# The opening of a decoder step: an early table load, matmuls on zeros, split weight pieces and two key tiles built side by side

## Chip, cores and metric

The kernel is one program on one core of a Trainium2 chip. Its five engines run their own instruction streams and meet at semaphores: TensorE (PE, the matmuls, with its weight loads as PEld), VectorE (DVE), ScalarE (ACT), GpSimd (POOL) and SyncE (SP, which here issues every DMA). The metric is the device time of one execution in microseconds (us); less is better.

## The reference, cut to what matters

One inference step of a trunk of two layers: 512 prompt tokens and 8 sequences of 8 new tokens, 576 tokens in all, with a model width of 1024. Layer 0 mixes tokens by sparse attention with three branches, layer 1 by a gated recurrence; each layer ends with an MLP and a gated projection. All matrices are in float32. The change touches only the first steps: the first norm and the first projections, the keys.

```python
def rmsnorm(x, g):
    xf = x.astype(jnp.float32)
    y = xf * lax.rsqrt(jnp.mean(xf * xf, axis=-1, keepdims=True) + RMS_EPS)
    return (y * g.astype(jnp.float32)).astype(x.dtype)
...
def nsa_project(h, pos, w_in):
    q, kv, gl = jnp.split(h @ w_in, [Q_DIM, Q_DIM + 6 * KV_DIM], axis=-1)
    q = rope(q.reshape(B, T, N_HEADS, HEAD_DIM), pos)
    kv = kv.reshape(B, T, 3, 2, KV_HEADS, HEAD_DIM)
    k = rope(kv[:, :, :, 0].reshape(B, T, 3 * KV_HEADS, HEAD_DIM), pos)
```

## The kernel before

**Layout.** The residual x lies transposed in SBUF as `X`, 8 tiles of 128 features by 576 tokens. A float32 product is made of three passes on numbers of lower precision: every operand is split into a high part (rounded on ACT) and a low part (the rest, by a subtraction on DVE), and a matmul adds hi·hi, hi·lo and lo·hi. `dense_steps` (L236 to L260) does this for one output tile of 128 columns: for each of 8 feature tiles k it issues six passes of 288 tokens, L251 for `wh`·`xh`, L254 for `wh`·`xl` and L257 for `wl`·`xh`. One output tile is 48 passes.

**Weights.** `piece` (L218) loads one 128x1024 block into `wr` (4 buffers), rounds it into `wh` on ACT (L212) and subtracts into `wl` (L229); `wh` and `wl` have 3 buffers each.

**The norm.** `norm_parts` (L327) makes `xh` on ACT (L332) and `xl` on DVE (L333) from `X` times the gain. `norm_square` squares on ACT (L342) and adds the squares into `ssq` (L344) on the engine that it is told. The factor 1/rms itself is not needed for the matmuls: it is applied to their results. It comes in two steps that are held in a list `late` and called between matmuls. `norm_sums` (L349) adds over the features by small matmuls (L355) and forms `RT`, the factor per token, by 12 short DVE instructions (L357, L321 to L326). `norm_spread` (L360) builds diagonal matrices on DVE and POOL (L370, L372), multiplies them by ones on PE (L373, L374), and copies the result to `R` on ACT (L375, L376).

**The key tiles.** The loop at L562 makes eight output tiles, m = 0 to 7, in pairs: compressed keys, compressed values, selected keys, window keys. Their results lie in PSUM in pair buffers `d`, of which there are three here. A finished tile is read out by `k_out`: values are multiplied by `R` (L464); keys go through `rope_out`, which copies quarters on ACT (L452), multiplies by the cosine table on DVE (L453), by the sine table on POOL (L454) and adds (L455). Both tables have first been multiplied by `R` on POOL (L568). So no key tile can leave PSUM before the spread norm is there.

**What sets the order.** The program is recorded in the order of the code, and a scheduler that goes by estimated times then places the instructions of each engine; buffers of a pool are handed out in that same estimate. Each engine runs its list strictly in order. SP issues DMAs in order too, over 8 completion semaphores in turn: a ninth DMA waits until the first has landed.

Of the kernel before, what the change touches and what calls it, by code (L numbers as in the profile page):

```python
# [39 lines left out]
BL = 1, 6  # L40
MID = 4
B0 = 3, 2
MAGIC = 0x5F3759DF


# [129 lines left out]
def program(tc, A, O):  # L175
# [20 lines left out]
    def pair():  # L196
        return psum["d"].tile([128, 2, 512], F32, name="d")

    def bank():
        return psum["s"].tile([128, 512], F32, name="s")  # L200
# [7 lines left out]
    def load(out, src):  # L208
        return nc.sync.dma_start(out, src)
# [7 lines left out]
    def piece(src, shape=(8, 128), lo_on=None, keep=None):  # L217

        n = int(np.prod(shape))
        raw = wp.tile([128, WCOL], F32, name="wr", bufs=4)  # L220
        if keep is not None:
            hi, lo = keep[:, :n], keep[:, n:2 * n]
        else:
            hi = wp.tile([128, WCOL], F32R, name="wh")
            lo = wp.tile([128, WCOL], F32R, name="wl")
        rs = raw[:, :n]
        load(rs, src)
        split_hi(hi[:, :n], rs)
        (lo_on or V).tensor_tensor(lo[:, :n], rs, hi[:, :n].bitcast(F32), op=OP.subtract)  # L229
        pat = "p (a b) -> p a b" if len(shape) == 2 else "p (a b c) -> p a b c"  # L230
        kw = dict(zip("abc", shape))
        return hi[:, :n].rearrange(pat, **kw), lo[:, :n].rearrange(pat, **kw)
# [27 lines left out]
    def dense(hi, lo, xh, xl, mid=None):  # L260

        o = pair()
        for k, _ in enumerate(dense_steps(hi, lo, xh, xl, (o[:, 0, :H2], o[:, 1, :H2]), pin=mid)):
            if k == mid:
                late()
        late()
        return o[:, :, :H2]
# [28 lines left out]
    X = hold["X"]  # L296
    gains = cst.tile([128, 7, KT], F32, name="gains")
    load(gains, A["gains"])
    load(X[:, 0], A["x"][:, 0])
    first = [piece(A["w_k"][0])]  # L300
    for k in range(1, KT):
        load(X[:, k], A["x"][:, k])
        if k == 2:
            first.append(piece(A["w_k"][1]))
    con = cst.tile([128, CONST.shape[1]], F32, name="con")
    C = lambda n: con[:, OFF[n][0]:OFF[n][0] + OFF[n][1]]
    ident = C("ident")
# [27 lines left out]
    def norm_square(m, on):  # L335

        X = hold["X"]
        if m == 0:
            sq = hold["ssq"] = cst.tile([128, NT], F32, name="ssq")
        else:  # L340
            sq = tmp.tile([128, NT], F32, name="t")
        S.activation(sq, X[:, m], AF.Square)  # L342
        if m:
            on.tensor_tensor(hold["ssq"], hold["ssq"], sq, op=OP.add)  # L344
# [42 lines left out]
    load(con, A["const"])  # L387
    V.tensor_copy(identb, ident)
    for m in range(KT):
        norm_square(m, G if m in (1, 4, 7) else V)  # L390
    norm_end()
    hold["late"].insert(0, lambda: None)

    def out_steps(src, oh, ol, ks, got, single=False):

# [29 lines left out]
    def nsa(after):  # L425
# [29 lines left out]
            on.tensor_tensor(out, t1, sw, op=OP.add)  # L455

        def k_proj(m):
            return dense(*(first[m] if m < 2 else piece(A["w_k"][m])), xh, xl, 1 if m == 1 else None)

        def k_out(p, out, rot):  # L460
            if rot:
# [97 lines left out]
        loads = comp_load(cd)  # L559
        outs = [(t[:, m], name) for t, name in ((kC, "o_kc"), (vC, "o_vc"), (kS, "o_ks"), (kW, "o_kw")) for m in range(2)]  # L560
        wait = []
        for m, (out, name) in enumerate(outs):  # L562
            wait.append((k_proj(m), out, name, m % 2))
            for _ in range((0, 0, 3, 3, 3, 3, 3, 1)[m]):
                next(loads, None)
            if m == 1:
                for i in range(2):
                    G.tensor_tensor(rope[:, i], rope[:, i], R, op=OP.mult)  # L568
            while wait and not hold["late"]:
                p, out, name, i = wait.pop(0)  # L570
                k_out(p, out, name != "o_vc")
                store(O[name][:, i], out)
# [975 lines left out]
```

## Time and profile before

| | us |
|---|---|
| median of 3 runs | 1835.22 |
| lowest, highest | 1832.96, 1835.82 |
| the profiled execution | 1833.71 |
| its span, first to last instruction | 1831.9 |
| PE busy in the span | 1768.1 (97%) |
| DVE, ACT, POOL busy | 971.0, 714.2, 479.7 |

The profile is of one execution, so its times are compared with its own 1833.71 us: 1.8 us lie outside the span. A timeline row gives the start, the duration, the engine, the source line, the operation with the tile written and the tiles read, the shape, the number of merged instructions, and in brackets how long the engine was idle before and what ended that. Matmuls overlap: two rows of PE that start 0.13 us apart may each last 0.30 us, so the distance between starts is the price of one.

### The profile page before, as it was taken

The page shows a single profiled execution, that of the slowest core. Times are in us where ns is not written, and L with a number is a line of the kernel's source. Part 1 is how long each engine was busy: PE and PEld are TensorE (multiplying, and loading weights), DVE is VectorE, ACT ScalarE, POOL GpSimd, SP SyncE. Part 2 cuts the span into 40 slices and gives each one's busy share as a digit, 9 for nine tenths or more (in the row PEclk, how much of TensorE's full clock was granted, in tenths as well). Part 3 has the DMA queues.
Part 4 walks back from the last instruction along what each step waited for, and adds up shares of the span by engine and source line. Part 5 has one row for each costly group of instructions (what it writes and reads, how often), then busy time and mean ns, then how long its engine had stood idle before and what let it go on. Part 6 is the DMA issues. An engine that isn't in the chain of part 4 may idle for free.

```text
span 1831.9 us, 31929 instructions
## 1 busy us (share of the span) xinstructions
PE 1768.1 (97%) x13016; PEld 1695.2 (93%) x13016; DVE 971.0 (53%) x1671; ACT 714.2 (39%) x1333; POOL 479.7 (26%) x463
## 2 busy tenths in 40 slices
PE   7999888989999999999999999999999999999997
PEld 7898777779999999999999999999899999999997
DVE  7644777665433334345666757667563333334564
ACT  5556687664332232313432323233243223131442
POOL 3536666652221110202112111211142102020121
PEclk9999999999999999999999999999999999999998
DMA  8333112313222222223231222221132222222311
GB/s 291 128 107 92 35 47 79 113 53 121 81 81 83 91 81 81 82 84 102 88 102 60 82 72 84 81 67 62 39 116 86 86 83 81 81 88 85 115 39 52
DMA packets 64917, 159.42 MB, mean 87 GB/s; under 512 B 8706, under 2 KB 26690, under 8 KB 64770
## 3 DMA queue, kind: packets, MB, share of 16 engines
q1 hardware_dynamic: 64770, 157.38, 26.9%
q8 instruction: 102, 1.67, 0.4%
q14 instruction: 45, 0.37, 0.1%
HBM read 142.33 MB, written 15.02 MB: 86 GB/s over the span
## 4 chain that ended last, share of the span: by engine, by line
PE 88%; DVE 5%; ACT 3%; DMA 1%; issue 1%; POOL 1%; SPq 0%; DVEq 0%; ACTq 0%; POOLq 0%
PE d L251 21%; PE d L254 21%; PE d L257 21%; PE s L1160 2%; PE s L889 1%; PE s L1404 1%; PE s L1408 1%; PE s L1407 1%; PE s L1227 1%; PE s L762 1%; PE s L1222 1%; PE s L845 1%; PE d L1042 1%; PE d L1043 1%; DMA wr<-p_g 1%
## 5 line engine op out<-in xcount | busy, mean ns | idle before, releaser
L212 ACT ACTIVATE wh<-wr 128x1024 fp32r<-128x1024 f32 (+3 forms) x227 | 231.8, 1023 | 764.9 <-PE d L254 635.7
L251 PE MATMUL d<-xh,wh 128*128 128x288 f32 x1776 | 506.1, 299 | 9.9 <-ACT wh L212 7.8
L254 PE MATMUL d<-xl,wh 128*128 128x288 f32 x1776 | 502.6, 298 | 1.9 <-DVE xl L333 1.9
L257 PE MATMUL d<-xh,wl 128*128 128x288 f32 x1776 | 385.2, 297 | 0.3 <-DVE wl L229 0.3
L229 DVE TENSOR_TENSOR wl<-wr,wh 128x1024 fp32r<-128x1024 f32 (+3 forms) x209 | 250.5, 1199 | 243.1 <-ACT wh L212 241.6
L251 PEld LDWEIGHTS d<-xh,wh 128*128 128x128 f32 x1776 | 335.8, 189 | 12.2 <-ACT wh L212 7.8
L254 PEld LDWEIGHTS d<-xl,wh 128*128 128x128 f32 x1776 | 336.1, 189 | 4.8 <-DVE xl L333 3.2
L257 PEld LDWEIGHTS d<-xh,wl 128*128 128x128 f32 x1776 | 286.8, 189 | 1.8 <-DVE wl L229 0.9
L251 PE MATMUL d<-hh,wh 128*128 128x288 f32 x1024 | 287.1, 295 | 0.0
L254 PE MATMUL d<-hl,wh 128*128 128x288 f32 x1024 | 286.8, 295 | 0.0
L1322 POOL TENSOR_TENSOR t<-t 128x576 f32<-128x576 f32 x64 | 104.8, 1637 | 504.0 <-ACT t L1320 504.0
L257 PE MATMUL d<-hh,wl 128*128 128x288 f32 x1024 | 217.9, 294 | 0.0
L254 PEld LDWEIGHTS d<-hl,wh 128*128 128x128 f32 x1024 | 192.4, 188 | 0.0
L251 PEld LDWEIGHTS d<-hh,wh 128*128 128x128 f32 x1024 | 192.3, 188 | 0.0
L257 PEld LDWEIGHTS d<-hh,wl 128*128 128x128 f32 x1024 | 164.2, 188 | 0.0
L1331 DVE TENSOR_TENSOR t<-d,R 128x576 f32<-128x576 f32 x64 | 48.5, 758 | 201.1 <-PE d L257 201.1
L344 POOL TENSOR_TENSOR ssq<-ssq,t 128x576 f32<-128x576 f32 x33 | 54.7, 1658 | 286.8 <-ACT t L342 283.4
L806 POOL TENSOR_SCALAR Eb<-Eb,sm,gate 128x512 f32<-128x512 f32 (+3 forms) x128 | 77.2, 620 | 35.9 <-DVE sm L852 22.8
L215 DVE TENSOR_TENSOR hl<-t,hh 128x576 fp32r<-128x576 f32 x64 | 48.6, 759 | 64.7 <-POOL t L1322 63.7
L1176 POOL TENSOR_TENSOR k<-k,T 128x256 f32<-128x256 f32 (+1 forms) x48 | 34.9, 728 | 183.0 <-PE s L1160 110.1
L850 ACT ACTIVATE Eb<-s,mx 128x512 f32<-128x512 f32 (+2 forms) x96 | 55.2, 582 | 30.5 <-DVE mx L848 29.1
L215 DVE TENSOR_TENSOR pl<-s,ph 128x512 fp32r<-128x512 f32 x80 | 53.1, 684 | 21.5 <-ACT ph L212 21.4
(398 smaller groups left out, 3180.2 us busy)
## 6 DMA issues: line engine op xcount, KB each, us to landing
wr<-w SPq DMA_DIRECT2D x128, 512.0 KB
wr<-p_g SPq DMA_DIRECT2D x16, 512.0 KB
X<-x SPq DMA_DIRECT2D x16, 288.0 KB
wr<-w_k SPq DMA_DIRECT2D x8, 512.0 KB
cd<-cache SPq DMA_DIRECT2D x16, 256.0 KB
wr<-w_c SPq DMA_DIRECT2D x8, 512.0 KB
wr<-w_q SPq DMA_DIRECT2D x8, 512.0 KB
wr<-w_o SPq DMA_DIRECT2D x8, 512.0 KB
```

Source lines behind the costliest of these rows:

```text
L212: S.activation(out, src, AF.Copy, **({} if scale is None else {"scale": scale}))
L215: (on or V).tensor_tensor(out, src, hi.bitcast(F32), op=OP.subtract)
L229: (lo_on or V).tensor_tensor(lo[:, :n], rs, hi[:, :n].bitcast(F32), op=OP.subtract)
L251: z = T.matmul(out[h], hi[:, k], xh[:, k, sl], start=k == 0, stop=False)
L254: T.matmul(out[h], hi[:, k], xl[:, k, sl], start=False, stop=False)
L257: T.matmul(out[h], lo[:, k], xh[:, k, sl], start=False, stop=k == nk - 1)
L344: on.tensor_tensor(hold["ssq"], hold["ssq"], sq, op=OP.add)
L806: G.tensor_scalar(e, e, r, gt3[:, j, h, 1 + br:2 + br], op0=OP.mult, op1=OP.mult)
L850: S.activation(E[:, r, :W], s[:, r - r0, :W], AF.Exp, bias=mx[:, r:r + 1], accum_out=sm[:, r:r + 1])
L1160: T.matmul(p[r, o // 2:e // 2], k[:, o:e], blk(q[:, o:e])[:, :, 1], start=True, stop=True)
L1322: G.tensor_tensor(r2, r, r, op=OP.mult)
L1331: V.tensor_tensor(two(t), p, two(R2), op=OP.mult)
```

## The change

Five edits, all ahead of the fourth key tile.

1. A tile `idle` of 128x512 bfloat16 is set to zero on DVE and multiplied by itself 11 times on PE (L305 of the new file), into a PSUM bank that nothing reads.
2. ACT copies one number (`dry`), so that its table is loaded ahead of the first wait for an input.
3. The first two weight pieces are loaded, rounded and subtracted in two halves of 512 columns (`halves`); the first halves of both come right behind the first tile of `X`, the second halves behind the third.
4. All additions into `ssq` go to DVE; three of seven were on POOL.
5. Key tiles 0 and 1 are computed together, feature tile by feature tile, into two pair buffers. `norm_sums` is called after them and `norm_spread` inside tile 2, behind its fifth feature tile; before, they were called inside and behind tile 1.

```diff
+    idle = tmp.tile([128, 512], BF, name="t")
+    V.memset(idle, 0.0)
+    z = bank()
+    for _ in range(WARM):
+        T.matmul(z, idle[:, :128], idle, start=True, stop=True)
+    dry = small.tile([128, 1], F32, name="dry")
+    G.memset(dry, 0.0)
+    S.activation(dry, dry, AF.Copy)
+    def halves(src):
+        raw = wp.tile([128, WCOL], F32, name="wr", bufs=4)
+        hi, lo = [wp.tile([128, WCOL], F32R, name=n) for n in ("wh", "wl")]
+        for i in range(2):
+            cs = slice(i * 512, i * 512 + 512)
+            load(raw[:, cs], src.rearrange("p k n -> p (k n)")[:, cs])
+            split_hi(hi[:, cs], raw[:, cs])
+            split_lo(lo[:, cs], raw[:, cs], hi[:, cs])
+            yield
...
+    parts = [halves(A["w_k"][m]) for m in range(2)]
     load(X[:, 0], A["x"][:, 0])
-    first = [piece(A["w_k"][0])]
     for k in range(1, KT):
+        if k in (1, 3):
+            next(parts[0])
+            next(parts[1])
         load(X[:, k], A["x"][:, k])
-        if k == 2:
-            first.append(piece(A["w_k"][1]))
...
-        norm_square(m, G if m in (1, 4, 7) else V)
+        norm_square(m, V)
     norm_end()
-    hold["late"].insert(0, lambda: None)
...
-            return dense(*(first[m] if m < 2 else piece(A["w_k"][m])), xh, xl, 1 if m == 1 else None)
+            return dense(*piece(A["w_k"][m]), xh, xl, 4 if m == 2 else None)
...
+        early = [pair() for _ in range(2)]
+        steps = [dense_steps(*first[m], xh, xl, (z[:, 0, :H2], z[:, 1, :H2])) for m, z in enumerate(early)]
+        for _ in range(KT):
+            for z in steps:
+                next(z)
+        late()
         for m, (out, name) in enumerate(outs):
-            wait.append((k_proj(m), out, name, m % 2))
+            wait.append((early[m][:, :, :H2] if m < 2 else k_proj(m), out, name, m % 2))
-            if m == 1:
+            if m == 2:
                 for i in range(2):
                     G.tensor_tensor(rope[:, i], rope[:, i], R, op=OP.mult)
```

The scheduler moves the instructions that follow. Three places are shown, as the built programs have them; the lines of the new file stand 27 to 33 lower.

PE at its start. Before (`d_184` is the pair of key tile 0, `wh_92` and `wl_93` its weights):

```order
L251 MATMUL d_184<-xh_118,wh_92 128x288
L254 MATMUL d_184<-xl_119,wh_92 128x288
L251 MATMUL d_184<-xh_118,wh_92 128x288
L254 MATMUL d_184<-xl_119,wh_92 128x288
L257 MATMUL d_184<-xh_118,wl_93 128x288 x2
```

Now (`t_90` is the tile of zeros, `s_92` the unread bank; `d_207` and `d_208` are the pairs of key tiles 0 and 1, with weights 109/110 and 115/116):

```order
L305 MATMUL s_92<-t_90 128x512
L252 MATMUL d_207<-xh_141,wh_109 128x288
L255 MATMUL d_207<-xl_142,wh_109 128x288
L252 MATMUL d_207<-xh_141,wh_109 128x288
L255 MATMUL d_207<-xl_142,wh_109 128x288
L252 MATMUL d_208<-xh_141,wh_115 128x288
L255 MATMUL d_208<-xl_142,wh_115 128x288
L252 MATMUL d_208<-xh_141,wh_115 128x288
L255 MATMUL d_208<-xl_142,wh_115 128x288
L258 MATMUL d_207<-xh_141,wl_110 128x288 x2
```

The eleven passes on zeros stand first, and each feature tile now gives twelve passes, six per key tile, where it gave six.

PE where the norm is spread, inside the third key tile (`d_348` before, `d_332` now; `t_308`, `t_313` and `t_368`, `t_373` are the diagonals from DVE and POOL, `s` the banks of the norm). Before:

```order
L254 MATMUL d_348<-xl_119,wh_343 128x288
L257 MATMUL d_348<-xh_118,wl_344 128x288 x2
L373 MATMUL s_303<-t_308,onesr_111 128x512
L374 MATMUL s_246<-t_308,onesr_111 128x64
L251 MATMUL d_348<-xh_118,wh_343 128x288
L254 MATMUL d_348<-xl_119,wh_343 128x288
L373 MATMUL s_303<-t_313,onesr_111 128x512
L251 MATMUL d_348<-xh_118,wh_343 128x288
L374 MATMUL s_246<-t_313,onesr_111 128x64
L254 MATMUL d_348<-xl_119,wh_343 128x288
```

Now:

```order
L255 MATMUL d_332<-xl_142,wh_327 128x288
L258 MATMUL d_332<-xh_141,wl_328 128x288 x2
L401 MATMUL s_363<-t_368,onesr_134 128x512
L402 MATMUL s_305<-t_368,onesr_134 128x64
L401 MATMUL s_363<-t_373,onesr_134 128x512
L402 MATMUL s_305<-t_373,onesr_134 128x64
L252 MATMUL d_332<-xh_141,wh_327 128x288
L255 MATMUL d_332<-xl_142,wh_327 128x288
```

The four spreading passes stood behind four feature tiles of the tile, with key passes between them; they now stand in a row behind five, and `norm_sums`, which stood inside tile 1, is now inside this same tile.

DVE where the first tiles are read out of PSUM. Before (`d_184` and `d_233` are key tiles 0 and 1, `d_348` is tile 2, the first value tile):

```order
L229 TENSOR_TENSOR wl_518<-wr_516,wh_517 128x1024
L453 SCALAR_TENSOR_TENSOR t_323<-d_184,rope_169 128x576
L464 TENSOR_TENSOR qT_181<-d_348,R_116 128x576
L453 SCALAR_TENSOR_TENSOR t_333<-d_233,rope_169 128x576
L455 TENSOR_TENSOR qT_181<-t_323,t_322 128x576
L229 TENSOR_TENSOR wl_613<-wr_611,wh_612 128x1024
L492 COPY wr_884<-qT_181 64x16x16 x4
L455 TENSOR_TENSOR qT_181<-t_333,t_332 128x576
```

Now (`d_207`, `d_208` are key tiles 0 and 1, `d_332` is tile 2):

```order
L400 TENSOR_TENSOR t_368<-con_133,rt0_364 128x64
L491 TENSOR_TENSOR qT_204<-d_332,R_139 128x576
L480 SCALAR_TENSOR_TENSOR t_431<-d_207,rope_192 128x576
L230 TENSOR_TENSOR wl_636<-wr_634,wh_635 128x1024
L480 SCALAR_TENSOR_TENSOR t_441<-d_208,rope_192 128x576
L482 TENSOR_TENSOR qT_204<-t_431,t_430 128x576
L519 COPY wr_907<-qT_204 64x16x16 x2
```

Tile 2 is now read ahead of tile 0. Before, the first pass of key tile 3 waits for DVE's reading of tile 0 (L453); now it takes the pair that tile 2 had, and waits for DVE's reading of tile 2 (L491). Further behind, the order is the same up to the attention blocks. There, from about 199 to 416 us in the trace before, PE's list is built otherwise in some 75 places; the passes are the same, and from there to the end the order is again the same.

## Rows read from the trace of the kernel before

**Rows 1.** The page, part 1: busy time of each engine, its share of the span and its instructions.
```profile
PE 1768.1 (97%) x13016; PEld 1695.2 (93%) x13016; DVE 971.0 (53%) x1671; ACT 714.2 (39%) x1333; POOL 479.7 (26%) x463
```

**Rows 2.** Busy time by stretch of the span (from:to, length, then PE, PEld, DVE, ACT, POOL busy with their counts, granted clock, DMA share, GB/s).
```profile
0.00:36.00 36.00, 25.77 (x163) 23.57 (x164) 23.79 (x41) 22.68 (x34) 11.36 (x15) 1.00 0.88 310
36.00:74.00 38.00, 38.00 (x283) 38.00 (x283) 25.90 (x37) 21.38 (x31) 17.35 (x10) 1.00 0.37 122
...
196.00:416.00 220.00, 198.96 (x1242) 162.55 (x1243) 147.65 (x294) 156.50 (x421) 142.25 (x196) 0.96 0.22 68
```

**Rows 3.** The timeline of ACT and PE up to the first matmul.
```profile
4.13 1.28 ACT L332 ACT_TABLE_LOAD   x1 [4.13 <-DMA X<-x]
5.43 0.77 ACT L332 ACTIVATE xh<-X,gains 128x576 fp32r<-128x576 f32 x1
6.11 0.67 ACT L342 ACTIVATE ssq<-X 128x576 f32<-128x576 f32 x1
...
6.68 1.04 ACT L212 ACTIVATE wh<-wr 128x1024 fp32r<-128x1024 f32 x1
...
7.77 0.61 PE L251 MATMUL d<-xh,wh 128*128 128x288 f32 x1 [7.77 <-ACT wh L212]
```

**Rows 4.** The timeline of SP: each of these issues waits for an earlier DMA to land, in this order the second tile of `X`, the third, and the second weight piece.
```profile
6.79 0.33 SPq L209 DMA_DIRECT2D con<-const  x1
...
8.07 0.33 SPq L209 DMA_DIRECT2D rope<-rope  x1
...
9.36 0.30 SPq L209 DMA_DIRECT2D pid<-pages  x1
```

**Rows 5.** The timeline of PE: neighbouring passes of one shape, early and a few us later.
```profile
8.42 0.44 PE L251 MATMUL d<-xh,wh 128*128 128x288 f32 x1
...
8.66 0.44 PE L254 MATMUL d<-xl,wh 128*128 128x288 f32 x1
...
12.76 0.29 PE L251 MATMUL d<-xh,wh 128*128 128x288 f32 x1
...
12.89 0.30 PE L254 MATMUL d<-xl,wh 128*128 128x288 f32 x1
```

**Rows 6.** The timeline of DVE, POOL and PE where `xl` and the sums of squares are made.
```profile
8.89 2.71 DVE L333 SCALAR_TENSOR_TENSOR xl<-X,gains,xh 128x576 fp32r<-128x576 f32 x2
...
9.04 1.95 POOL L344 TENSOR_TENSOR ssq<-ssq,t 128x576 f32<-128x576 f32 x1 [7.39 <-ACT t L342]
...
17.49 0.40 PE L254 MATMUL d<-xl,wh 128*128 128x288 f32 x1 [0.85 <-DVE xl L333]
...
18.37 0.81 DVE L333 SCALAR_TENSOR_TENSOR xl<-X,gains,xh 128x576 fp32r<-128x576 f32 x1
...
19.10 0.75 DVE L344 TENSOR_TENSOR ssq<-ssq,t 128x576 f32<-128x576 f32 x1
...
19.77 0.81 DVE L333 SCALAR_TENSOR_TENSOR xl<-X,gains,xh 128x576 fp32r<-128x576 f32 x1
```

**Rows 7.** The timeline of PE, DVE and POOL from the norm's sums to the first pass of key tile 3 (the row at 27.95 is the first pass of key tile 2).
```profile
21.93 1.28 PE L355 MATMUL s<-onesr,ssq 128*128 128x1 f32 x10 [0.36 <-POOL ssq L344]
...
23.24 0.16 DVE L357 TENSOR_SCALAR na<-s 128x5 f32<-128x5 f32 x1 [0.21 <-PE s L355]
...
23.52 1.23 DVE L229 TENSOR_TENSOR wl<-wr,wh 128x1024 fp32r<-128x1024 f32 x1
...
24.66 0.16 DVE L322 TENSOR_SCALAR RT<-nwi 128x5 int32<-128x5 int32 x1
...
27.55 1.07 DVE L372 TENSOR_TENSOR t<-con,rt 128x64 fp32r<-128x64 f32 x1
...
28.50 0.29 POOL L372 TENSOR_TENSOR t<-con,rt 128x64 fp32r<-128x64 f32 x1
...
27.95 0.30 PE L251 MATMUL d<-xh,wh 128*128 128x288 f32 x1
...
31.15 0.40 PE L373 MATMUL s<-t,onesr 128*128 128x512 f32 x1
...
34.45 0.76 DVE L453 SCALAR_TENSOR_TENSOR t<-d,rope 128x576 f32<-128x576 f32 x1 [4.25 <-POOL rope L568]
...
35.36 0.37 PE L251 MATMUL d<-xh,wh 128*128 128x288 f32 x1 [0.15 <-DVE t L453]
```

**Rows 8.** The timeline of PE at two later waits, and the granted clock (third number from the end) of the stretches behind them.
```profile
77.75 0.64 PE L513 MATMUL d<-cl,wh 128*128 128x322 f32 x1 [3.02 <-DVE cl L215]
...
80.80 0.30 PE L512 MATMUL d<-ch,wh 128*128 128x322 f32 x1
...
296.38 0.44 PE L752 MATMUL s<-con,dE 128*128 128x128 f32 x2 [2.11 <-POOL dE L746]
...
76.00:80.00 4.00, 2.25 (x8) 2.25 (x9) 2.98 (x5) 2.41 (x4) 1.55 (x1) 0.66 0.75 258
...
294.00:298.00 4.00, 1.59 (x13) 1.06 (x11) 2.50 (x8) 3.77 (x16) 4.00 (x10) 1.00 0.19 66
```

**Rows 9.** Who waited for whom on PE from 196 to 416 us (total us, times, longest), and the timeline of PE at one place there: a score product's pass on the high part of the keys (L845) and the pass on the low part behind it (L846).
```profile
PE s L845 <- ACT Eb L850: 1.8, 3, 1.1
...
218.77 0.48 PE L845 MATMUL s<-kh,qs 128*128 128x512 f32 x1
219.09 0.40 PE L846 MATMUL s<-kl,qs 128*128 128x512 f32 x1
```

More of the change, by code (lines that the diff above doesn't have):

```diff
@@ L42 @@
 B0 = 3, 2
+WARM = 11
 MAGIC = 0x5F3759DF
@@ L298, in program @@
     load(gains, A["gains"])
+    idle = tmp.tile([128, 512], BF, name="t")
[15 more added lines that the diff above has]
+            yield
+        first.append([z[:, :1024].rearrange("p (k n) -> p k n", k=8) for z in (hi, lo)])
+        yield
+    first = []
+    parts = [halves(A["w_k"][m]) for m in range(2)]
     load(X[:, 0], A["x"][:, 0])
-    first = [piece(A["w_k"][0])]
     for k in range(1, KT):
+        if k in (1, 3):
+            next(parts[0])
+            next(parts[1])
         load(X[:, k], A["x"][:, k])
-        if k == 2:
-            first.append(piece(A["w_k"][1]))
+    for z in parts:
+        next(z)
     con = cst.tile([128, CONST.shape[1]], F32, name="con")
@@ L561, in nsa @@
         wait = []
+        early = [pair() for _ in range(2)]
+        steps = [dense_steps(*first[m], xh, xl, (z[:, 0, :H2], z[:, 1, :H2])) for m, z in enumerate(early)]
+        for _ in range(KT):
+            for z in steps:
+                next(z)
+        late()
         for m, (out, name) in enumerate(outs):
-            wait.append((k_proj(m), out, name, m % 2))
+            wait.append((early[m][:, :, :H2] if m < 2 else k_proj(m), out, name, m % 2))
             for _ in range((0, 0, 3, 3, 3, 3, 3, 1)[m]):
                 next(loads, None)
-            if m == 1:
+            if m == 2:
                 for i in range(2):
```

## The prediction

> **What bounds the kernel now.** I read the page first: PE is busy 97% of the span [rows 1]. That share says where the end is set, but it is a mean; the windows by stretch show which stages differ. From 36 to 74 us PE is busy for the whole 38.00 us, in the attention blocks from 196 to 416 us for 198.96 of 220, and in the first 36 us for only 25.77 [rows 2]. So a microsecond saved at the start moves everything behind it, as long as the next waits there are waits for things that PE itself brought forward.
>
> In the opening the reader should see four losses. First, PE starts at 7.77, when the first weight piece is rounded, and ACT got to that late: it waited for the first tile of X until 4.13 and only then loaded its table for 1.28 us [rows 3]. [...] Third, PE waits for `xl`, for instance until 17.49; two `xl` on DVE take 2.71 us while POOL adds a square at 9.04, against 0.81 each with POOL idle [rows 6]. Fourth, key tile 3 cannot start before tile 0 has left PSUM, which takes the spread norm: it starts at 35.36, having waited 0.15 for DVE [rows 7]. That last row is the one to hold on to: **the chain sums, norm, spread, reading out ended there together with PE's own work.** Whatever speeds up PE alone is stopped by it.
>
> PE's own work up to that point is three tiles of 48 passes at 0.133, 19.2, and about 2 for the norm: 21.2 of 35.36 us. So 14 us is the most that any edit here can bring; the rest is to be shown.
>
> **The table load, the zeros, the halves.** With the table loaded early, `xh` of the first tile can start at 4.13 instead of 5.43, a gain of 1.30 on ACT [rows 3]. From there I walk ACT's new list. One `xh` costs 0.68 (5.43 to 6.11) and one square 0.57 (6.11 to 6.68) [rows 3]; rounding half a piece, 512 columns, I estimate at 0.52, a little under the square's 576. The halves' landing is not in the trace. From below it cannot be before 4.13, the landing of the tile ahead of them; from above, the two halves are together as many bytes as the whole piece that stood in the same place, and the tile behind that had landed by 6.79 [rows 4]. I take 5.4 and 6.0. The second tile of X then lands by 6.79, the third by 8.07, the second halves by 9.36, as before, because the same bytes are ahead of each [rows 4]. ACT so waits for inputs three times, and its 1.30 shrinks: second `xh` 6.8, third 8.1, halves until 10.3, and from then 1.25 per tile, the last `xh` at 15.3 and the last square over at 16.6.
>
> The zeros cost PE nothing, since it has nothing else to do until 5.9, when the first half is rounded. Eleven passes of 512 columns at the lower level cost 11 × 0.24 × 512/288 = 4.7 us; from about 1.2 they end at 5.9. Rows show the rise to the higher level 4.5 us after the first pass [rows 3, 5] and, after another wait, 3.05 us after it (77.75 to 80.80) [rows 8]; both fit in ahead of the keys. I take the higher level from the first key pass on.
>
> **The squares on DVE.** POOL's three additions leave; DVE gets three at 0.67 (19.10 to 19.77) and makes each `xl` in 0.73 (18.37 to 19.10) [rows 6]. Nothing waits for POOL here any more. A half subtraction I estimate at 0.60, from 1.14 for a whole one (23.52 to 24.66) [rows 7]. DVE is done with the second halves at 11.5 and with the fourth `xl` at 12.2; then four `xl`, three additions and some 0.4 of short instructions put the last `xl` at 17.5, and the last two additions put the sum of squares at 18.9.
>
> **Two tiles side by side.** Each feature tile now feeds twelve passes, 1.6 us, which covers DVE's 1.40 per tile; that is what the interleaving is worth. PE has done 38 of the 96 passes when the fourth `xl` arrives at 12.3; the other 58 take 7.7, so tiles 0 and 1 end at 20.0. Before, tile 2 started at 27.95 [rows 7] with the sums behind it; now the sums (1.1) are still to come. **PE's own gain is 27.95 − 20.0 − 1.1 = 6.8 us.**
>
> **The new end of the chain.** The sums stand behind four passes of tile 2, at 20.5, against 21.93: 1.4 us earlier [rows 7]. DVE's list behind them is the same, one whole weight subtraction among the short steps included, so the diagonals, ready at 28.62 on DVE and 28.79 on POOL [rows 7], are now ready at 27.2 and 27.4. Before, PE came for them only at 31.15, and the 2.4 us of slack hid the norm. Now PE comes at 20.0 + 30 × 0.133 + 1.1 = 25.1 and waits in its list until 27.4, with the rest of tile 2 queued behind. It is through the spread at 27.7, the last 18 passes take 2.4, results stand 0.2 later: 30.3. Then a second wait that was not there: tile 3 takes tile 2's pair, so DVE must first read tile 2, 0.76 as for the row at 34.45, and hand over, 0.15 [rows 7]. Tile 3 starts at 31.2 instead of 35.36: **a gain of 4.1 us.** The two waits, about 2.1 and 1.0, are covered by nothing.
>
> Behind this the lists are the same until 199 us, PE is never idle from 36 to 74 [rows 2], and later waits there hang on work that moves along. DMAs: the two more issues on SP come while ACT waits anyway; no store or cache load that follows is needed within 10 us. The attention order changes; without a reason for a sign I set it at zero. From the profiled execution the sum is 1833.7 − 4.1 = 1829.6; it lies 1.5 below the median of the runs shown, so the forecast for a median is 1835.2 − 4.1 = 1831.1.
>
> **Rivals.** *More arrives.* PE's whole 6.8 gets through if the norm chain is shorter than I have it, or the new attention order sheds a tenth of its 21.0 us without PE work [rows 2], 2.1. For it: DVE and POOL collide less. Against it: the two waits stand in the built order. 6.8 gives 1828.4.
>
> *The clock falls again.* The two new waits lie 2.5 us apart. After a wait of 3.02 the granted clock was 0.66 over four us and the next 3.05 us ran at half pace; after one of 2.11 it stayed at 1.00 [rows 8]. If it falls, those 3.05 us cost 1.4: the gain is 2.7, 1832.5. Each wait is at most as long as the one that did no harm, which speaks against it.
>
> *The zeros do not do what they are for.* If the clock rises only at about 12, PE has done 24 passes by then instead of 38 and ends the two tiles at 22.2; all behind is 2.2 later: gain 1.9, 1833.3. [...]
>
> *Slower.* At 218.77 a score's low pass follows its high pass at once, at 219.09 [rows 9]. In the new order 21 key-side passes, 2.8 us, stand between the high pass of the third score and the low passes of all three, so the maxima and exponentials of that group come 2.8 later. If PE runs out of other work meanwhile, as it did for 1.8 us in three places there [rows 9], that is lost. It decides from two such places fully exposed: 5.6 − 4.1 = 1.5 slower, 1836.7. For it: the waits in that stretch are many. Against it: the scheduler filled the gap with work that has to be done anyway.
>
> *Nothing.* A later wait that does not move with PE (a cache page, a store) eats all: 1835.
>
> **How the numbers follow.** Forecast 0.42, more arrives 0.19, clock 0.12, zeros 0.07, slower 0.13, nothing 0.07. A measurement of this kernel can tell about 0.2%, 3.7 us, from no change, and the forecast of 4.1 lies close to that edge. Faster by more than that: 0.28 of the forecast's 0.42, nearly all of "more arrives", a little of the rest, 0.49. Slower by more: less than half of "slower", with a remainder, 0.07. Within: 0.44. The range, 1826.5 to 1835.8, reaches from "more arrives" with a gain in the attention blocks to "nothing" with the noise of the runs; outside are the slower case and the extremes of the first, under 0.2.
>
> **What would show it.** Right: eleven passes on zeros from about 1.2 to 5.9; the first key pass near 5.9 at 0.13 spacing; the sums near 20.5; a wait of PE near 25 to 27 for the diagonals, another of about 1 us behind tile 2 for DVE; tile 3 near 31.2. Wrong: tile 3 at 29 or below (the chain did not bind), a granted clock under 1.00 before 40 us, or PE time in 196 to 416 us that differs by more than 2 us from 198.96 plus its waits. If the halves land much later than 5.4 and 6.0, all from 5.9 on moves, but the chain from 12 us on less, since the second halves set it.

## The result, and the profile after

The changed kernel takes 1851.09 us (median; 1849.89 to 1853.56), the kernel before 1835.52. The ratio is 1.0089, with a 95% interval of 1.0073 to 1.0105: **slower by 0.9%**, where 0.2% faster was forecast. The profiled execution took 1853.56, with a span of 1851.6. Two far slower executions are left out of the figures further down, one of run e8 (8247 us) and one of the kernel before that was timed beside run e12 (2157 us).

The same instruction can be followed through both traces, since behind the opening nearly everything is there in both. Where it starts later, time was lost between it and the landmark ahead of it.

| landmark | before | changed | difference |
|---|---|---|---|
| PE, first pass of key tile 3 | 35.36 | 33.73 | -1.63 |
| PE, first pass of the first compressed product | 67.34 | 72.21 | +4.87 |
| DVE, a maximum at the start of the attention blocks (L848, now L881) | 198.66 | 202.67 | +4.01 |
| DVE, first step of the second norm (L357, now L385) | 470.79 | 487.35 | +16.56 |
| DVE, first reading of a projection in layer 1 (L1074, now L1107) | 954.83 | 972.72 | +17.89 |
| DVE, in the last steps (L1413, now L1446) | 1812.03 | 1831.60 | +19.57 |

So the opening gains 1.6, some 5.6 are lost between there and 199 us, 12.5 in the attention blocks, 1.3 in the MLP of layer 0, and 1.7 towards the end.

**The opening** is as planned up to 25 us. PE's timeline, the rows that answer to [rows 3, 5, 7]:

```profile
1.20 4.41 PE L305 MATMUL s<-t 128*128 128x512 bf16 x11 [1.20 <-DVE t L302]
6.13 0.40 PE L252 MATMUL d<-xh,wh 128*128 128x288 f32 x1 [0.53 <-ACT wh L213]
6.37 0.29 PE L255 MATMUL d<-xl,wh 128*128 128x288 f32 x1
6.50 0.29 PE L252 MATMUL d<-xh,wh 128*128 128x288 f32 x1
...
13.16 0.40 PE L255 MATMUL d<-xl,wh 128*128 128x288 f32 x1 [0.54 <-DVE xl L361]
...
21.52 1.17 PE L383 MATMUL s<-onesr,ssq 128*128 128x1 f32 x10
...
27.29 0.47 PE L401 MATMUL s<-t,onesr 128*128 128x512 f32 x1 [1.05 <-DVE t L398]
28.17 0.30 PE L402 MATMUL s<-t,onesr 128*128 128x64 f32 x1 [0.41 <-DVE t L400]
...
29.06 0.44 PE L252 MATMUL d<-xh,wh 128*128 128x288 f32 x1
29.30 0.44 PE L255 MATMUL d<-xl,wh 128*128 128x288 f32 x1
...
33.73 0.40 PE L252 MATMUL d<-xh,wh 128*128 128x288 f32 x1 [0.92 <-DVE qT L491]
```

The zeros end at 5.61, before the first half is rounded (PE waits for that until 6.13), and from 6.37 the first key passes stand 0.13 apart, where they stood 0.24 apart in [rows 5]; run e7 below, without the zeros, has 0.24 there again. The two new waits are there too: 1.05 and 0.41 for the diagonals, 0.92 for DVE behind tile 2. But behind the first two, from 29.06, the passes are 0.24 apart. The window shows the granted clock (the third number from the end) at 0.61 there:

```profile
28.00:32.00 4.00, 3.83 (x18) 3.79 (x19) 0.12 (x1) 0.71 (x2) 2.68 (x4) 0.61 0.77 212
```

The 18 passes left of tile 2 take 4.2 us, until 32.8, in place of 2.4, and key tile 3 starts 2.5 later than forecast.

**The first compressed product** waits, PE's timeline:

```profile
72.21 0.64 PE L539 MATMUL d<-ch,wh 128*128 128x322 f32 x1 [6.31 <-DVE t L480]
```

Before, the same pass started at 67.34 without a wait. L480 is the reading of a key tile out of PSUM, on DVE, and DVE's timeline shows why it is late:

```profile
63.01 0.76 DVE L480 SCALAR_TENSOR_TENSOR t<-d,rope 128x576 f32<-128x576 f32 x1 [4.05 <-ACT t L479]
63.68 5.88 DVE L519 COPY wr<-qT 64x256 f32<-64x256 f32 x8
69.59 1.90 DVE L482 TENSOR_TENSOR kk<-t 128x576 f32<-128x576 f32 x1
71.41 0.74 DVE L480 SCALAR_TENSOR_TENSOR t<-d,rope 128x576 f32<-128x576 f32 x1
```

Key tile 7 is read at 71.41, behind eight copies that take 5.88 us together. That list is the same in both kernels. What differs is which PSUM pair each tile was given; the built programs say:

```
key tile        0  1  2  3  4  5  6  7   first compressed product
before:  pair   A  C  B  A  B  C  A  B   A   (waits for tile 6)
changed: pair   A  C  B  B  A  C  B  A   A   (waits for tile 7)
```

Behind the key tiles PSUM is divided anew, and the product gets the first pair of the new division, A, whoever holds it. Because tile 3 now takes tile 2's pair, the rotation is shifted and A belongs to the tile that was just made.

**The attention blocks** take 12.6 longer for the same work. The windows are laid 4.0 later at the start and 16.6 later at the end, as the landmarks around them, so that they hold the same passes; first before, then the changed kernel (length, then PE busy with its count):

```profile
199.00:422.00 223.00, 202.78 (x1277) 166.66 (x1276) 147.49 (x293) 156.99 (x421) 142.62 (x193) 0.97 0.24 74
```

```profile
203.00:438.60 235.60, 211.93 (x1277) 174.06 (x1276) 149.76 (x294) 157.53 (x421) 138.71 (x193) 0.93 0.23 71
```

Both hold 1277 passes; PE is busy 9.2 longer, at a lower granted clock (0.93 in place of 0.97), and idle 3.4 longer. The place that the prediction named is one of those that lose:

```profile
222.59 0.40 PE L878 MATMUL s<-kh,qs 128*128 128x512 f32 x1
...
223.85 0.48 PE L878 MATMUL s<-kh,qs 128*128 128x512 f32 x1
224.17 0.33 PE L252 MATMUL d<-xh,wh 128*128 128x288 f32 x1
...
226.87 0.30 PE L252 MATMUL d<-xh,wh 128*128 128x288 f32 x1
227.00 0.39 PE L879 MATMUL s<-kl,qs 128*128 128x512 f32 x1
```

The key passes between high and low pass hold the low pass back until 227.00, where before it followed after 0.32 [rows 9]. ACT, which makes the exponentials of these scores, is idle for 3.49, where it was idle for 0.97 before:

```profile
228.23 0.69 ACT L883 ACTIVATE Eb<-s,mx 128x512 f32<-128x512 f32 x1 [3.49 <-DVE mx L881]
```

ACT's work just ahead of this exponential is 4.3 later than before, the exponential itself 7.0: this place costs 2.7. The largest single step lies further on. Before, PE made the scores of a later sequence (`dk`) ahead of the products with the values of an earlier one (`dv`):

```profile
367.40 1.05 PE L729 MATMUL d<-dk,qo 128*128 128x264 f32 x4
...
369.35 1.14 PE L762 MATMUL s<-dE,dv 128*128 128x128 f32 x8
```

In the changed kernel the scores stand behind, and PE later waits 2.21 for POOL, which scales the exponentials made from them (0.27 before):

```profile
379.23 1.05 PE L795 MATMUL s<-dE,dv 128*128 128x128 f32 x8
...
382.13 0.71 PE L762 MATMUL d<-dk,qo 128*128 128x264 f32 x2
...
393.52 0.44 PE L785 MATMUL s<-con,dE 128*128 128x128 f32 x2 [2.21 <-POOL dE L779]
```

From ACT's last exponential of one sequence to the first of the next it is 3.70 before (366.40 to 370.10) and 9.08 now (377.55 to 386.63), so this place alone costs 5.4 of the 12.5.

**The MLP** has the same order and no waits, and still its passes come more slowly. From 560 to 860 us PE is busy without a gap in both; it makes 2269 passes before (first of the two rows) and 2261 now (second):

```profile
560.00:860.00 300.00, 300.00 (x2269) 300.00 (x2268) 119.45 (x133) 80.53 (x97) 36.05 (x22) 1.00 0.28 85
```

```profile
560.00:860.00 300.00, 300.00 (x2261) 300.00 (x2261) 114.08 (x125) 77.78 (x92) 34.92 (x22) 1.00 0.27 83
```

Eight passes are 1.06 us. Layer 1's MLP does the same towards the end, first before, then now:

```profile
1460.00:1720.00 260.00, 260.00 (x1966) 260.00 (x1965) 101.63 (x112) 68.31 (x81) 28.57 (x18) 1.00 0.27 84
```

```profile
1460.00:1720.00 260.00, 260.00 (x1960) 260.00 (x1959) 96.83 (x107) 62.99 (x74) 27.45 (x17) 1.00 0.27 84
```

Between DVE's step at 1349.61 before (1366.18 now) and that at 1720.65 (1738.52), it loses another 1.3. In the built program the only thing that differs there is the address: the small tile `dry` of the early table load makes its pool 64 bytes larger, and the operands that lie behind it (the second norm's output, the hidden parts, layer 1's) move by that. Runs e9 to e11 below measure what goes with this tile.

### The profile page after: what moved, and what is told of

It is laid out like the page before. It is cut to its first block, busy times and chain, and to the rows that moved or that the text cites. A ratio compares the mean times of both kernels' runs of the same rounds, so it can differ in the third digit from the quotient of the medians.

```text
span 1851.6 us, 31956 instructions
## 1 busy us (share of the span) xinstructions
PE 1784.5 (96%) x13027; PEld 1708.2 (92%) x13027; DVE 971.7 (52%) x1677; ACT 715.0 (39%) x1336; POOL 468.8 (25%) x461
## 4 chain that ended last, share of the span: by engine, by line
PE 89%; DVE 6%; ACT 2%; issue 1%; POOL 1%; DMA 0%; SPq 0%; DVEq 0%; ACTq 0%; POOLq 0%
PE d L252 21%; PE d L255 21%; PE d L258 21%; PE s L1193 2%; PE s L922 2%; PE s L1437 1%; PE s L1441 1%; PE s L1440 1%; PE s L878 1%; PE s L795 1%; PE s L905 1%; PE s L1255 1%; PE s L906 1%; PE d L1075 1%; PE d L1076 1%
## 5 line engine op out<-in xcount | busy, mean ns | idle before, releaser
L213 ACT ACTIVATE wh<-wr 128x1024 fp32r<-128x1024 f32 (+6 forms) x229 | 232.1, 1016 | 764.3 <-PE d L255 631.3
L230 DVE TENSOR_TENSOR wl<-wr,wh 128x1024 fp32r<-128x1024 f32 (+5 forms) x207 | 248.0, 1199 | 245.6 <-ACT wh L213 244.2
L372 POOL TENSOR_TENSOR ssq<-ssq,t 128x576 f32<-128x576 f32 x30 | 48.6, 1621 | 271.9 <-ACT t L370 271.7
```

The lines of the kernel that those rows point to most:

```text
L213: S.activation(out, src, AF.Copy, **({} if scale is None else {"scale": scale}))
```

## The experiments

Theory: two large losses that have nothing to do with the length of the opening, an occupied pair at 66 us and a worse attention order, and a smaller one, that goes with the tile that moves operands by 64 bytes. Main rival: one loss only, the late start and low clock at 72 us (0.50 from 72 to 76 us in the changed kernel), which put the attention work out of step. In the tables below "attention" is the difference between a run and the kernel before that arises from the landmark at 198.66 to that at 470.79; for the changed kernel it is 12.55. Landmarks are of one profiled execution per run; medians and ratios are of several, each beside its own executions of the kernel before.

### Pair and order, one at a time

Run e1 makes one tiny write into pair A, so that the product gets the next one:

```diff
+            if kind == 0:
+                V.memset(pair()[:, 0, :8], 0.0)
             z = pair()
```

> The changed kernel, and one VectorE instruction more: a write of 8 numbers into the PSUM pair that the first compressed product would have got, which is the pair of key tile 7. The product then takes the next pair, that of key tile 6, and TensorE's order in the attention blocks stays that of the changed kernel. Theory (two losses, a pair still occupied at 66 us and a worse attention order): the wait of 6.3 us before the first compressed product goes, the median falls from 1851.1 by about 5.7 to 1845, and the 12.5 us that the attention stretch lost remain. Rival 1 (one loss: the late and half-clocked start at 72 us shifts the attention work against ScalarE, GpSimd and the cache loads, and that is what costs there, whatever the order): the median falls by all of 18, to 1833. Rival 2 (the wait is absorbed by the next one behind it): no change, 1851.

Run e2 calls the spread behind the eighth feature tile of tile 2; by this alone the scheduler makes the old attention order, and the pairs stay wrong:

```diff
-            return dense(*piece(A["w_k"][m]), xh, xl, 4 if m == 2 else None)
+            return dense(*piece(A["w_k"][m]), xh, xl, 7 if m == 2 else None)
```

> The changed kernel with the norm's spread behind the eighth feature tile of key tile 2 in place of the fifth. TensorE's list from key tile 3 to the end is then, place for place, that of the kernel before, while the pairs are still those of the changed kernel, so that the first compressed product must wait for key tile 7. Theory (two losses): the attention stretch gets its 12.5 us back, the wait at 66 us of about 6 stays: 1851.1 - 12.5 = 1838.6, perhaps 2 less since key tile 3 can start near 31.5 instead of 33.7. Rival 1 (the late start costs the attention stretch its time, whatever the order): 1849 to 1851.

Run e3 has both edits.

> The edits of the two runs before it together: spread behind the eighth feature tile, and the first compressed product in the pair of key tile 6. Theory: neither loss, the opening's gain comes through; key tile 3 near 31.5 is 3.9 earlier than before, 1831.6, the clock after the waits permitting; 1831 to 1833. Rival 1: also near 1832, so this run alone does not decide. Rival 3 (the opening's gain is lost again further on, at the compressed products, which wait for GpSimd and VectorE): 1835.5.

Run e4 calls the spread one feature tile earlier; tile 3 then takes tile 0's pair, and order and pairs are both the old ones.

```diff
-            return dense(*piece(A["w_k"][m]), xh, xl, 4 if m == 2 else None)
+            return dense(*piece(A["w_k"][m]), xh, xl, 3 if m == 2 else None)
```

> The changed kernel with the norm's spread behind the fourth feature tile of key tile 2 in place of the fifth. By this alone key tile 3 takes the pair of tile 0, the first compressed product finds the pair of key tile 6 and not of 7, and TensorE's list from key tile 3 on is that of the kernel before. Theory: both losses gone, while TensorE waits 0.8 longer for the diagonals; key tile 3 starts at 32.5 to 34, 1.4 to 2.9 earlier than before: 1832.5 to 1834. Rival 1: the same. Rival 4 (the early pieces in themselves are worth nothing, and the 1.6 us gain at key tile 3 is all waiting moved on): 1835.5.

| run | product waits for | order | median | ratio to before (95%) | attention |
|---|---|---|---|---|---|
| changed kernel | tile 7 | new | 1851.09 | 1.0089 (1.0073 to 1.0105) | +12.55 |
| e1 | tile 6 | new | 1845.94 | 1.0049 (1.0031 to 1.0066) | +10.15 |
| e2 | tile 7 | old | 1842.74 | 1.0041 (1.0028 to 1.0055) | +1.84 |
| e3 | tile 6 | old | 1835.34 | 0.9994 (0.9985 to 1.0004) | +3.34 |
| e4 | tile 6 | old | 1834.41 | 0.9995 (0.9983 to 1.0007) | +0.08 |

The pair is worth 5.2 (changed kernel to e1) and 7.4 (e2 to e3), the order 8.4 (changed kernel to e2, which also starts tile 3 earlier by 2.1) and 10.6 (e1 to e3). The kernel before, timed beside e1 to e4, was 1.0 slower than beside the changed kernel (1836.50 and 1835.52), so the two prices from the changed kernel are rather 1 larger. The rival falls: e1 has no late start at 72 us and still loses 10.15 in the attention, e2 has it and loses 1.84. e2 keeps the wait, and pays for it as the changed kernel does:

```profile
71.53 0.64 PE L539 MATMUL d<-ch,wh 128*128 128x322 f32 x1 [6.31 <-DVE t L480]
```

while in e3 the same pass follows the key passes at once:

```profile
63.30 0.43 PE L258 MATMUL d<-xh,wl 128*128 128x288 f32 x2
63.57 0.31 PE L541 MATMUL d<-ch,wh 128*128 128x322 f32 x1
```

e2 came out 4.1 above the 1838.6 expected and e3 3.7 above 1831.6: the opening's gain did not all reach the end. That is the subject of the runs further down.

### Which edit is to blame

Run e5 is the kernel before with the squares on DVE, nothing else:

```diff
-        norm_square(m, G if m in (1, 4, 7) else V)
+        norm_square(m, V)
```

> The kernel before with one of the five edits alone: all additions into the sum of squares on VectorE. No zeros, no early table, no halves, no side by side tiles. In the built program key tile 3 takes the pair of tile 2 as in the changed kernel, the first compressed product gets the pair of key tile 7, and the attention blocks have a third order (54 places off that of the kernel before). Theory: the wait of about 6.3 us at the first compressed product appears here too, worth 5 to 7; the attention order adds 0 to 12: 1841 to 1855 against 1836.5. Rival (it is the new opening that hurts, this edit is harmless, and the three additions cost VectorE 2 us at most): 1835 to 1838.5.

Measured: 1841.16, ratio 1.0028 (1.0019 to 1.0037), the wait of 6.33 is there, and the attention adds 4.5:

```profile
73.01 0.64 PE L512 MATMUL d<-ch,wh 128*128 128x322 f32 x1 [6.33 <-DVE t L453]
```

So a harmless looking edit of three additions is enough to turn the pairs round. The side by side tiles are not needed for it. Whether it is also what turns them in the changed kernel is not shown: e4 keeps the additions on DVE and has the old pairs.

### The zeros and the early table

Run e6 is the kernel before with the zeros and the `dry` activation alone:

```diff
+    idle = tmp.tile([128, 512], BF, name="t")
+    V.memset(idle, 0.0)
+    z = bank()
+    for _ in range(11):
+        T.matmul(z, idle[:, :128], idle, start=True, stop=True)
+    dry = small.tile([128, 1], F32, name="dry")
+    G.memset(dry, 0.0)
+    S.activation(dry, dry, AF.Copy)
     load(X[:, 0], A["x"][:, 0])
```

> The kernel before with the early table load and the eleven matmuls on zeros alone; pairs and attention order are those of the kernel before. Theory (the zeros raise the clock ahead of the first key pass, and the opening is then bound by the inputs and the norm): first key pass near 6.5 at a spacing of 0.13, the norm's sums 0.5 to 1.3 earlier than 21.93, key tile 3 as much earlier than 35.36, and all of it kept: 0.5 to 1.3 under the kernel before. Rival (the zeros do nothing, key passes start at 0.24 spacing): sums and key tile 3 within 0.3.

Measured: 1839.06, ratio 1.0009 (1.0000 to 1.0018), not faster and rather slower; both theories missed the time. The first key passes, from 7.06, do stand 0.13 apart, and the sums come at 21.05, 0.9 earlier, as the theory has it. But the granted clock falls twice, in the windows (0.72, and 0.75 and 0.50):

```profile
6.00:12.00 6.00, 4.57 (x18) 3.75 (x19) 5.27 (x6) 6.00 (x9) 1.94 (x1) 0.72 1.00 382
14.00:24.00 10.00, 8.40 (x43) 7.41 (x41) 8.74 (x14) 4.69 (x7) 3.75 (x2) 0.75 1.04 399
24.00:28.00 4.00, 4.00 (x18) 4.00 (x18) 3.63 (x15) 0.00 (x0) 0.76 (x1) 0.50 0.72 225
```

With one key tile at a time PE still waits for `xl` (1.5 in two waits, 1.9 in three before), and in this execution, with passes 0.24 apart from 24 to 28 us, key tile 3 started at 38.10, 2.7 later than before. That the zeros cost time over several executions is not shown: the small tile, below, is in this run too, and alone it has the ratio 1.0010.

Run e7 is e4 with no zeros at all:

```diff
-WARM = 11
+WARM = 0
```

> The run with the spread one feature tile earlier, without the eleven matmuls on zeros. Theory: key passes run at a spacing of 0.24 until about 11 to 12, tiles 0 and 1 end 1.5 to 2.2 later, the sums and key tile 3 with them, so key tile 3 starts near 33.6 to 34.3. The attention order differs again (53 places off the kernel before, 54 off the changed one), pairs as in the kernel before: 1835 to 1848 by how good that order is. Rival (the first passes run at 0.13 without the zeros, or the waits for inputs hide it): key tile 3 within 0.4 of 32.1.

Measured: 1834.21, ratio 0.9990 (0.9980 to 0.9999). Key tile 3 starts at 31.84, with the zeros (e4) at 32.07, so the rival is right. The passes do run 0.24 apart until 10.6, 4.6 us after the first at 6.03, as in the kernel before (7.77 to about 12.3); but then PE has no more waiting to do:

```profile
10.04 0.45 PE L255 MATMUL d<-xl,wh 128*128 128x288 f32 x1
10.28 0.49 PE L258 MATMUL d<-xh,wl 128*128 128x288 f32 x2
10.61 0.29 PE L255 MATMUL d<-xl,wh 128*128 128x288 f32 x1
10.74 0.30 PE L252 MATMUL d<-xh,wh 128*128 128x288 f32 x1
```

What the zeros win there PE waits for a little later: e4 goes on at 13.24, after a wait of 0.56 for `xl`, and e7 at 13.14 without one. The attention order of e7 is a fourth one; its profiled execution lost 3.3 there, but at 1837.96 that execution was 3.8 above the run's median.

### The wait for the diagonals, and the 64 bytes

Run e8 is e4 with passes whose result is overwritten, to keep PE working until the diagonals are there:

```diff
         o, o2 = bank(), hold["sums"][:, 64:128]
+        if hold["X"] is X:
+            for _ in range(14):
+                T.matmul(o[:, :H2], onesr, xh[:, 0, :H2], start=True, stop=True)
```

> The run with the spread one feature tile earlier, and 14 passes of 288 columns whose result is overwritten put where TensorE waits 1.84 us for the diagonals (1.9 us at a spacing of 0.133). Pairs and attention order are those of the kernel before. Theory (where such waits let the clock fall, that costs up to 1.6 us, in some executions and not in others): key tile 3 stays at 32.1, the median comes to 3 us under the kernel before, with less spread than 1832.2 to 1842.5. Rival (the clock is not the matter, the 14 passes only delay): the same as without them, 2 under, or 0.3 slower.

Measured: 1834.77, ratio 0.9987 (0.9978 to 0.9996). Alone it is not to be told from e4. The passes did not all go where they were meant: nine stand right behind the norm's sums, at 22.48, and five at 26.42, at the end of the key passes that come ahead of the spread. Together they close the first wait; a second one of 0.49 stays.

Run e9 is the kernel before with the small tile, which is set to zero and not used:

```diff
+    dry = small.tile([128, 1], F32, name="dry")
+    G.memset(dry, 0.0)
```

> The kernel before, and nothing but the small tile that the early table load uses: allocated where the changed kernel has it and set to zero once on GpSimd. No engine's order changes behind that, TensorE's list and all pairs are those of the kernel before; but the tiles of layer 0's second norm, of the MLP's hidden parts and of layer 1 lie 64 bytes per partition further. Theory (the passes of the MLP ran at 132.8 ns a pass instead of 132.4 in every run that has this tile, 2261 instead of 2269 passes from 560 to 860 us, because of where the operands lie): 2261 passes there, and 2 to 4 slower than the kernel before. Rival (the pace differs by execution or by what TensorE did earlier): 2269 passes, no difference.

Runs e10 and e11 are e4 and the changed kernel with that tile taken from a pool whose buffers are there anyway:

```diff
-    dry = small.tile([128, 1], F32, name="dry")
+    dry = tmp.tile([128, 1], F32, name="t")
```

> The run with the spread one feature tile earlier, with the early table load writing into one of the buffers that are there anyway, so that no tile moves. Order and pairs as in the kernel before. Theory (as for the small tile alone): 2269 passes from 560 to 860 us, and with the 3.3 us of the opening kept to the end: 1831.5 to 1833.5, against 1836.7. Rival: as with the tile, 1834.4.

> The changed kernel with the early table load writing into one of the buffers that are there anyway. Theory: 2 to 4 less than the changed kernel's 1851.1, 1847 to 1849; its pair of key tile 7 and its attention order stay. Rival: 1851.

The window of the MLP, of e9 and of e11:

```profile
560.00:860.00 300.00, 300.00 (x2261) 300.00 (x2261) 117.64 (x130) 79.90 (x95) 36.03 (x22) 1.00 0.28 85
```

```profile
560.00:860.00 300.00, 300.00 (x2269) 300.00 (x2268) 114.12 (x126) 78.44 (x94) 34.89 (x22) 1.00 0.28 84
```

2261 passes with the tile, 2269 without, in these two and in all the other runs (2260 in e2, which has it). The theory's count of the passes holds. In the time e9 is 1.0010 (1.0001 to 1.0019), 0.2 to 3.5 us; e11 is 1849.68, by the medians 1.4 under the changed kernel, but by the ratios (1.0073 and 1.0089) 2.9, and by the profiled spans (1849.0 and 1851.6) 2.6. The landmarks say where: in all nine profiled runs with the tile layer 0's MLP, from 470.79 to 954.83, loses 1.3, and from 1349.61 to 1720.65, layer 1's MLP, 1.3 again; the four without (e5, e10, e11, e12) lose nothing in either. So the tile costs 2.6. That the place of the operands is what slows the passes fits these runs; how it would act is not shown.

e10, at 1834.05 and 0.9987 (0.9978 to 0.9996), is hardly below e4. In the profiled e10 all went as in e4 up to 28 us; then the granted clock fell (0.61 from 28 to 32 us), and key tile 3 starts at 33.61 in place of 32.07: about half the gain is gone. (e4 and e10 ran on two chips; e2 and e3, compared further down, on one.) The windows of e10 and of e4, after the same two waits, 1.84 and 0.42 in e10, 1.84 and 0.41 in e4:

```profile
28.00:32.00 4.00, 3.67 (x17) 3.63 (x18) 1.03 (x2) 2.96 (x6) 2.68 (x4) 0.61 0.76 215
```

```profile
28.00:32.00 4.00, 3.73 (x27) 3.63 (x27) 0.97 (x2) 3.03 (x6) 2.68 (x4) 1.00 0.85 234
```

Run e12 puts together e4, e8 and e10.

> The changed kernel with what the runs so far point to: the spread one feature tile earlier (pairs and attention order as in the kernel before), no tile moved by the early table load, and the wait for the diagonals filled with 14 passes of 288 columns whose result is overwritten. Theory: the gain of 3.3 at key tile 3 without a fall of the clock behind the wait, less what later falls of the clock take: 1832.5 to 1834, under the run without the filling by 0.5 to 1.4. Rival (later falls of the clock eat it): 1834.

Measured: 1831.78, ratio 0.9974 (0.9963 to 0.9984): **3 to 7 us faster than the kernel before**. e7, e8 and e10 lie under the kernel before too, but their intervals end at 0.9999 and 0.9996; e12 is the only version that is clear of that edge. Its granted clock behind the filled wait stays at 1.00, as it did in e4 without the filling:

```profile
28.00:32.00 4.00, 3.61 (x26) 3.57 (x27) 1.05 (x2) 2.90 (x6) 2.68 (x4) 1.00 0.84 235
```

## Why the prediction was wrong

**Right.** The zeros end before the first half, and the key passes behind them stand 0.13 apart from 6.37 (0.24 without the zeros, e7); the first pass comes at 6.13 (5.9 forecast), the fourth `xl` at 13.16 (12.3), the sums at 21.52 (20.5), PE has the last of the diagonals at 28.17 (27.4), and the waits stand where the built order put them, 1.05 and 0.41 for the diagonals (2.1 forecast) and 0.92 for DVE (1.0). Of the lateness 0.9 is the second halves and the fourth `xl`, and the sums pass it on. That PE's pace alone does not set key tile 3 is right, and e7 shows it: its first passes stand 0.24 apart and the tile starts at 31.84, against 32.07 in e4. What the prediction calls the lower and the higher level are, in the rows, these two spacings, 0.24 and 0.13 [rows 5].

**The first step that failed** is "the clock falls again", held as a rival at 0.12 with the argument that each wait is at most as long as the one of 2.11 that did no harm [rows 8]. Waits of 1.05 and 0.41 stand ahead of the fall here (to 0.61), and in e1 and e11 as well, where the passes are 0.24 apart from 29.88 and 29.85: 18 passes took 4.2 and not 2.4, which with 1.0 of late inputs and diagonals, less 0.2 for a shorter readout, made the gain 1.6 in place of 4.1. One harmless wait was a sample of one. The runs show that the same wait goes either way. Behind tile 2 PE waits 2.30 in e2 and in e3, until 31.64 and 31.58; the next window of e2, then of e3:

```profile
32.00:36.00 4.00, 4.00 (x21) 4.00 (x21) 2.53 (x3) 0.91 (x2) 3.92 (x4) 0.63 0.94 346
```

```profile
32.00:36.00 4.00, 4.00 (x32) 4.00 (x31) 2.55 (x3) 0.86 (x2) 3.92 (x4) 1.00 0.92 341
```

Near equal histories ended differently in these two, at 0.63 and 1.00, and in e10 and e4, at 0.61 and 1.00; no run shows why.

**The second** is "Behind this the lists are the same until 199 us [...] and later waits there hang on work that moves along". The lists are the same; the buffers behind the names are not. The prediction did see that tile 3 takes tile 2's pair and priced that one handover; it did not carry the rotation on to tile 7. A pair that is still occupied is a wait that no order shows. It measured 5.2 to 7.4 in the time, and 5.6 between the landmarks in the trace.

**The third** is "The attention order changes; without a reason for a sign I set it at zero". It measured 8 to 11 in the time and 12.5 in the trace, the largest term of all. The rival "slower" had named the mechanism and a true place of it (the low passes at 227.00, which cost 2.7 where it said 2.8), but with 5.6 in all and a chance of 0.13; the place that costs 5.4 it did not see. A reason for a sign can be argued, though no run shows it: in an order in which PE is busy 90% of the time, with many short waits on ACT and POOL, there may be more ways to get worse than better. Four orders were met in these runs: that of before, and three others that cost 3.3 (e7), 4.5 (e5) and 10.2 to 12.5 (the changed kernel's); none was better. The old order in other runs varied from 0.1 to 3.3, so that the two cheaper ones can hardly be told from it. How the scheduler comes from an earlier opening to another attention order was not tried; that it depends on small things (three additions, one feature tile, the zeros) was.

**The fourth** is a term that the prediction does not have at all: the small tile, 2.6.

The sum as it came out, by the landmarks of the profiled execution: 1829.6 + 2.5 (key tile 3 at 33.73, not 31.2) + 5.6 (from there to 199 us, the pair) + 12.6 (attention) + 1.3 (layer 0's MLP) + 1.7 (behind it) = 1853.3, against 1853.56.

The zeros' own price was judged wrongly too. The prediction let PE end tiles 0 and 1 2.2 later without them; in e7 the sums stand at 21.38, in e4 at 21.62, because PE, with its first passes 0.24 apart, just waits less (not at all ahead of 13.14, where e4 waits 0.56 until 13.24). They are worth nothing here.

**Left open:** why PE makes 2261 passes and not 2269 where the operands lie 64 bytes further, and what lets the granted clock fall or not after the same wait. Of the 1.7 us that the changed kernel loses behind 955 us 1.3 go with the tile; the rest is a gain of 1.3 around 1300 us and a loss of 1.7 behind 1720, and both stretches differ by 2 to 3 us among the profiled runs, with the tile and without. How much of e12's gain is the filling and how much the tile that no longer moves anything is open as well, since by the time each alone (e8, e10) is not to be told from e4.

## What to carry to other kernels

Where a scheduler and pools decide, a change at the start is a change everywhere: besides the order, compare which buffer each tile gets, at the next place where a pool is divided anew, and follow the rotation to its end. When an edit elsewhere shuffles the order of a busy stretch, do not set that at zero without a reason: here none of three new orders was better, and the worst cost 8 to 11 us. Nudging a call by one position may restore the old one (e4). Work that makes an engine faster early on is worth nothing if the engine waits behind it anyway (key tile 3 starts at 32.07 with the zeros and at 31.84 without), and a small tile is best taken from buffers that exist: one of its own cost 2.6 us here.

## What the runs showed of the hardware

Behind the waits of these runs the granted clock, over the next 4 us, does not go by the wait's length: 1.84 and 0.41 left it at 1.00 once (e4) and 1.84 and 0.42 at 0.61 once (e10), 2.30 at 1.00 once (e3) and 0.63 once (e2), while behind the shorter 1.05 and 0.41 or 0.42 the passes stood 0.24 apart in all three runs that have them (from 29.06 in the changed kernel, at 0.50 from 29 to 32 us; from 29.88 in e1, at 0.50 from 30 to 32; from 29.85 in e11). In the first microseconds of e7 the granted clock in the profile's rows reads 1.00 while the passes stand 0.24 apart, so that the spacing, not that column, shows the pace there:

```profile
6.00:10.60 4.60, 4.57 (x19) 4.57 (x20) 3.71 (x6) 3.77 (x7) 0.00 (x0) 1.00 1.01 381
```

With the operands 64 bytes further PE made 2261 passes from 560 to 860 us (changed kernel, e9) where it made 2269 (kernel before, e11), and 1960 from 1460 to 1720 us (the same two) where it made 1966 (kernel before, e11), with no wait, at a granted clock of 1.00.
